# DeltaNet keys normed by the diagonal of their products, and one shared product for the last 16 tokens of eight heads

## The chip, the cores and the metric

The kernel runs on one core of a Trainium2 chip. The metric is device microseconds of one execution; lower is better. The engines are named as in the profile: PE (matrix products), PEld (its weight loads), DVE (vector), ACT (activation functions and copies), POOL, and SP, which issues most DMAs.

## The reference, cut to what matters

The block is one decoder layer on 272 tokens (16 meta tokens and 256 others), all in float32. One of its two token mixers is a chunked gated DeltaNet with 16 key and query heads and 32 value heads of 128 channels. The change touches only this part:

```python
def l2norm(x):
    return x * lax.rsqrt(jnp.sum(x * x, axis=-1, keepdims=True) + EPS)

qkv = jax.nn.silu(causal_dwconv(jnp.concatenate([q, k, v], axis=-1), conv_w)).astype(f32)
q, k, v = jnp.split(qkv, [GDN_QK_W, 2 * GDN_QK_W], axis=-1)
q = jnp.repeat(l2norm(q.reshape(B, L, GDN_QK_HEADS, Dh)), rep, axis=2) * (Dh ** -0.5)
k = jnp.repeat(l2norm(k.reshape(B, L, GDN_QK_HEADS, Dh)), rep, axis=2)
...
kk = jnp.einsum('bhid,bhjd->bhij', kc, kc)
lower = jnp.where(strict, bc[..., :, None] * kk * decay, 0.0)
...
attn = jnp.where(incl, jnp.einsum('bhid,bhjd->bhij', qc, kc) * decay, 0.0)
```

## The kernel before, in words

**The stream of weights.** Nearly all time goes to products of the activations with 376 weight tiles of 128 x 2048 (1 MB each). `Stream.load` fetches a tile on SP's queue into `wraw` (3 buffers). For each half of a tile ACT rounds it to `whi` (L149, 5 buffers) and DVE takes the rest to `wlo` (L157, 4 buffers). PE then runs 24 products of 256 to 272 columns for that half, into a PSUM tile `acc`. All matrix products are recorded at line 227 (helper `MM`), vector operations of two tensors at L230 (helper `TT`), activations at L243 (helper `ACT`).

**The background.** Everything else, the DeltaNet too, is written as generators that a list `bg` holds. `gemm` calls `bg.tick(EV)` ahead of the 24 products of a half and `bg.tick(PE)` behind them. At each tick up to five of the generators go one step. So what a generator does between two `yield`s lands either ahead of a half's products (on ACT, DVE, POOL and SP) or behind them (on PE). Each engine then runs its own instructions in the order in which they were written, and may run ahead of the others as far as data and buffers allow.

**PSUM.** The background has five PSUM tiles, `BP()` (named `bp`). Where a sixth is asked for, its first writer waits until the reader of an older one is done.

**The part that changes.** `gen_kq(h)` runs once for each of the 16 key heads, two at a time: heads 0 to 7 while the attention heads finish, at 362 to 446 us; heads 8 to 15 at 700 to 850 us. For keys (272 tokens) and queries (258) alike it squares (ACT), splits the squares into a rounded part `sqh` (ACT) and a rest `sql` (DVE), adds them up over the channels with two products by ones (PE, 272 or 258 columns), takes Ln and Exp (ACT), and multiplies (DVE). Then come the products: keys by keys (`a`, 272, 144 and 16 columns) and queries by keys (`b`, 258, 144 and 16). The products of 16 columns are for the last 16 tokens, from the third chunk. ACT copies all to `kq[h]` and `kq3`, POOL copies the diagonal 32 x 32 blocks to `ckk`.

`gen_inv(b)` runs once for eight heads. It writes `ckk` and `kq3` to memory and reads them back in another layout, inverts the triangular blocks on DVE, and writes the results for `gen_pair`, which computes the value heads in pairs.

Of the kernel before, what the change touches and what calls it, by code (L numbers as in the profile page):

```python
# [14 lines left out]
P = 128  # L15
# [192 lines left out]
def build(tc, x, w, cst, prm, out):  # L208
    nc = tc.nc
    with ExitStack() as ctx:  # L210
# [507 lines left out]
        kq3 = inv.tile([P, 8, 2, 16], F, name="kq3")  # L718
        ktl = inv.tile([P, 2, 8, 16], F, name="ktl")
        kk_dram = dram.tile([8, 2, 4, 32, 32], F, name="kk_dram")  # L720
        k3_dram = dram.tile([8, 16, 16], F, name="k3_dram")
        t_dram = [dram.tile([16, 2, 4, 32, 32], F, name=f"t_dram{b}") for b in range(2)]
        u_dram = [dram.tile([16, 2, 4, 32, 32], F, name=f"u_dram{b}") for b in range(2)]
        q3_dram = dram.tile([8, 16, 16], F, name="q3_dram")
# [41 lines left out]
        def gen_kq(h):  # L766
            k, q = raw.pop(("k", h)), raw.pop(("q", h))
            both = ((k, L, None, R("kqs")), (q, NQ, K("lnd"), R("kqs")))
            for t, n, _, s in both:
                ACT(s[:, :n], t[:, :n], AF.Square)  # L770
            yield EV
            parts = [split(s, n) for t, n, _, s in both]
            for t, n, b, s in both:
                yield PE
                p = BP()
                sums(p[:, :n], parts.pop(0))
                yield EV
                ACT(s[:, :n], p[:, :n], AF.Ln, bias=eps)
                ACT(s[:, :n], s[:, :n], AF.Exp, scale=-0.5, bias=0.0 if b is None else b)
            yield EV  # L780
            for t, n, _, s in both:
                TT(t[:, :n], t[:, :n], s[:, :n], OP.mult)
            del both, s, t
            yield EV
            while sum(("head", 2 * j + 1) not in done for j in kq) == 8:
                yield EV
            yield PE
            kq[h] = kqp.tile([P, 2, 416], F, name="kq", tag="kq")
            c = kq[h]
            a = BP()  # L790
            MM(a[:, 0:272], k[:, 0:128], k)
            MM(a[:, 272:416], k[:, 128:256], k[:, 128:272])
            MM(a[:, 416:432], k[:, 144:272], k[:, 256:272])
            yield EV
            yield from until(*[("inv", h // 8 - 1)] if h > 7 else [])
            ACT(c[:, 0, :], a[:, :416])
            ACT(kq3[96:128, h % 8, 0, :], a[96:128, 416:432])
            yield PE
            b = BP()
            MM(b[:, 14:272], k[:, 0:128], q[:, :NQ])  # L800
            MM(b[:, 272:416], k[:, 128:256], q[:, 114:258])
# [12 lines left out]
        def gen_inv(b):  # L814
# [4 lines left out]
            gb = inv.tile([P, 32], F, name="gb", tag="gb")  # L819
            nb = inv.tile([P, 32], F, name="nb", tag="nb")  # L820
# [12 lines left out]
            nc.sync.dma_start(out=k3_dram.rearrange("h j i -> j h i"), in_=kq3[112:128, :, 0, :])  # L833
            nc.sync.dma_start(out=q3_dram.rearrange("h j i -> j h i"), in_=kq3[112:128, :, 1, :])
# [6 lines left out]
            kkt = R("kkt")  # L841
            ACT(kkt[:, :256], p[:, :256])
            yield EV
            for d in range(2):
# [3 lines left out]
                nc.sync.dma_start(out=p3[h8].rearrange("p a b -> p (a b)"),  # L848
                                  in_=k3_dram.rearrange("h j i -> h (j i)"))
                nc.sync.dma_start(out=q3[h8].rearrange("p a b -> p (a b)"),  # L850
                                  in_=q3_dram.rearrange("h j i -> h (j i)"))
# [14 lines left out]
            for n, l, kk, g, be in both:  # L866
                ACT(l, l, AF.Exp)
# [7 lines left out]
            for n, l, kk, g, be in both:  # L875
# [4 lines left out]
            for n, l, kk, g, be in both:  # L880
# [574 lines left out]
```

## Time and profile before

| | |
|---|---|
| median of 3 runs | 2428.78 us (2428.12 to 2429.44) |
| the profiled execution's own time | 2428.07 us |
| its span, first to last instruction | 2426.4 us |
| PE busy | 2388.0 us (98%) |
| DVE, ACT, POOL busy | 1665.0, 1280.3, 455.0 us |
| mean granted clock of PE | 0.994 |

Busy time is the union of an engine's instructions. Products overlap on PE: a record lasts longer than the distance to the next one's start, so what a product costs is read from starts, not from durations. The span is 1.7 us shorter than the execution's own time.

### The profile page before, as it was taken

What the parts mean: (1) busy time and instruction counts of PE and PEld (TensorE: products, weight loads), DVE (VectorE), ACT (ScalarE), POOL (GpSimd) and SP (SyncE); (2) the same over time, 40 slices, a digit from 0 to 9 for tenths busy, and PEclk for the clock granted to TensorE, in tenths of its full rate; (3) what the DMA queues carried; (4) which work ended last, traced back from release to release, by engine and by line L of the source; (5) the groups of instructions that cost most, each with busy time, mean ns of one, the idle gap of its engine ahead of it and who ended that gap; (6) DMA issues with size and microseconds to landing.
All of it is one profiled execution on the core that took longest, in us unless ns stands there. A gap on an engine that the chain in (4) does not pass through costs nothing.

```text
span 2426.4 us, 48160 instructions
## 1 busy us (share of the span) xinstructions
PE 2388.0 (98%) x19870; PEld 2366.3 (98%) x19870; DVE 1665.0 (69%) x2653; ACT 1280.3 (53%) x2010; POOL 455.0 (19%) x620
## 2 busy tenths in 40 slices
PE   9999999999999999999999999999999999999997
PEld 8999999999999999999999999899999999999997
DVE  7777775796787597776665554597764777557755
ACT  6333568556767746666574544454444444334453
POOL 1767001424431134333000001210000000000012
PEclk9999999999999999999999999999999999999998
DMA  6445444564443466445676556435555455545552
GB/s 261 169 163 191 147 141 138 176 212 146 162 165 128 158 201 207 154 151 168 215 264 222 186 193 217 173 139 184 181 191 189 176 179 187 191 175 191 175 190 105
DMA packets 113836, 434.38 MB, mean 179 GB/s; under 512 B 34256, under 2 KB 63440, under 8 KB 66128
## 3 DMA queue, kind: packets, MB, share of 16 engines
q1 hardware_dynamic: 112320, 430.25, 50.9%
q8 instruction: 156, 2.56, 0.4%
q10 hardware_dynamic: 1296, 1.06, 0.1%
q14 instruction: 64, 0.52, 0.1%
HBM read 415.74 MB, written 15.52 MB: 178 GB/s over the span
## 4 chain that ended last, share of the span: by engine, by line
PE 92%; DVE 4%; ACT 3%; issue 1%; POOL 0%; DMA 0%; SPq 0%; DVEq 0%; ACTq 0%; POOLq 0%
PE acc L227 83%; PE bp L227 8%; DVE wlo L157 1%; DVE acc L230 1%; ACT whi L149 0%; ACT L243 0%; ACT sq_h L243 0%; DVE pr L230 0%; DVE tm L230 0%; ACT kqs L243 0%; PE bp L994 0%; POOL ro L230 0%; DMA wraw<-in_w_dram 0%; DVE xr L230 0%; ACT L954 0%
## 5 line engine op out<-in xcount | busy, mean ns | idle before, releaser
L157 DVE TENSOR_TENSOR wlo<-wraw,whi 128x1024 fp32r<-128x1024 f32 x747 | 932.8, 1251 | 296.7 <-PE acc L227 142.5
L149 ACT ACTIVATE whi<-wraw 128x1024 fp32r<-128x1024 f32 x747 | 786.9, 1058 | 639.6 <-PE acc L227 527.5
L227 PE MATMUL acc<-xh,whi 128*128 128x258 f32 (+3 forms) x2592 | 753.7, 291 | 5.4 <-ACT whi L138 5.4
L227 PE MATMUL acc<-xh,wlo 128*128 128x258 f32 (+3 forms) x2592 | 736.0, 284 | 0.4
L227 PE MATMUL acc<-xl,whi 128*128 128x258 f32 (+3 forms) x2592 | 733.1, 285 | 0.0
L227 PEld LDWEIGHTS acc<-xh,whi 128*128 128x128 f32 x2592 | 488.8, 189 | 7.8 <-ACT whi L138 5.4
L227 PEld LDWEIGHTS acc<-xh,wlo 128*128 128x128 f32 x2592 | 488.1, 188 | 1.3 <-DVE wlo L157 0.7
L227 PEld LDWEIGHTS acc<-xl,whi 128*128 128x128 f32 x2592 | 486.1, 188 | 1.0
L227 PE MATMUL acc<-uh,whi 128*128 128x258 f32 x1520 | 430.8, 284 | 4.4 <-ACT uh L243 2.9
L227 PE MATMUL acc<-uh,wlo 128*128 128x258 f32 x1520 | 432.5, 285 | 0.0
L227 PE MATMUL acc<-ul,whi 128*128 128x258 f32 x1520 | 429.4, 284 | 2.1 <-DVE ul L233 1.8
L227 PEld LDWEIGHTS acc<-uh,whi 128*128 128x128 f32 x1520 | 291.1, 192 | 5.2 <-ACT uh L243 3.3
L227 PEld LDWEIGHTS acc<-ul,whi 128*128 128x128 f32 x1520 | 288.1, 190 | 3.6 <-DVE ul L233 3.6
L227 PEld LDWEIGHTS acc<-uh,wlo 128*128 128x128 f32 x1520 | 289.4, 190 | 0.0
L227 PE MATMUL acc<-acth,wlo 128*128 128x256 f32 x768 | 215.9, 281 | 0.0
L227 PE MATMUL acc<-actl,whi 128*128 128x256 f32 x768 | 215.7, 281 | 0.0
L227 PE MATMUL acc<-acth,whi 128*128 128x256 f32 x768 | 215.3, 280 | 0.0
L227 PEld LDWEIGHTS acc<-acth,wlo 128*128 128x128 f32 x768 | 145.0, 189 | 0.0
L227 PEld LDWEIGHTS acc<-acth,whi 128*128 128x128 f32 x768 | 144.8, 189 | 0.0
L227 PE MATMUL acc<-oh,whi 128*128 128x258 f32 x512 | 144.8, 283 | 0.0
L227 PEld LDWEIGHTS acc<-actl,whi 128*128 128x128 f32 x768 | 144.8, 188 | 0.0
L227 PE MATMUL acc<-oh,wlo 128*128 128x258 f32 x512 | 144.6, 282 | 0.0
(325 smaller groups left out, 3610.4 us busy)
## 6 DMA issues: line engine op xcount, KB each, us to landing
wraw<-in_w_dram SPq DMA_DIRECT2D x371, 1024.0 KB
grow_h<-g_dram SPq DMA_DIRECT2D x32, 136.0 KB
s_o<-o_h SPq DMA_DIRECT2D x32, 129.0 KB
back<-s_o SPq DMA_DIRECT2D x32, 129.0 KB
wraw<-in_w_dram SPq DMA_DIRECT2D x5, 512.0 KB
s_ao<-ao SPq DMA_DIRECT2D x16, 129.0 KB
s_ga<-gate SPq DMA_DIRECT2D x16, 129.0 KB
s_gg<-gate SPq DMA_DIRECT2D x16, 129.0 KB
```

The source lines that it names most:

```text
L149: self.nc.scalar.activation(self.h[s], self.part(s), AF.Copy)
L157: self.nc.vector.tensor_tensor(out=lo, in0=self.part(s), in1=hi.bitcast(F), op=OP.subtract)
L227: nc.tensor.matmul(o, lhsT=l, rhs=r, start=start, stop=stop)
L230: (eng or nc.vector).tensor_tensor(out=o, in0=a, in1=b, op=op)
```

## The change

The keys are no longer multiplied by their norm ahead of the products. Square, split, sums, Ln, Exp and multiplication are done for the queries alone. The products of the raw keys are taken, and the sum of squares of each key is read off the diagonal of keys by keys: DVE multiplies the two diagonal blocks by the identity and reduces them. ACT makes `rk` of it, one factor for each token, and puts it in as the scale of the copies from PSUM, one copy for each of the two chunks of rows (four copies of a head instead of two). That scales rows only; the factor of the columns goes into `ntok` (POOL) and, for the inversion, into one more multiplication.

The products of 16 columns go. POOL copies the last 16 tokens of keys and queries of eight heads side by side into `last`, and `gen_inv` takes one product of 128 x 256 of it; the 16 x 16 blocks on its diagonal are what is wanted, and are picked out by the DMA's access pattern (`same`). `rk` travels to the inversion's layout through memory (`rk_dram`, `r3_dram`).

```diff
         def gen_kq(h):
             k, q = raw.pop(("k", h)), raw.pop(("q", h))
-            both = ((k, L, None, R("kqs")), (q, NQ, K("lnd"), R("kqs")))
-            for t, n, _, s in both:
-                ACT(s[:, :n], t[:, :n], AF.Square)
-            yield EV
-            parts = [split(s, n) for t, n, _, s in both]
-            for t, n, b, s in both:
-                yield PE
-                p = BP()
-                sums(p[:, :n], parts.pop(0))
-                yield EV
-                ACT(s[:, :n], p[:, :n], AF.Ln, bias=eps)
-                ACT(s[:, :n], s[:, :n], AF.Exp, scale=-0.5, bias=0.0 if b is None else b)
-            yield EV
-            for t, n, _, s in both:
-                TT(t[:, :n], t[:, :n], s[:, :n], OP.mult)
-            del both, s, t
-            yield EV
+
+            s = R("kqs")
+            ACT(s[:, :NQ], q[:, :NQ], AF.Square)
+            yield EV
+            parts = split(s, NQ)
+            yield PE
+            p = BP()
+            sums(p[:, :NQ], parts)
+            del parts
+            yield EV
+            ACT(s[:, :NQ], p[:, :NQ], AF.Ln, bias=eps)
+            ACT(s[:, :NQ], s[:, :NQ], AF.Exp, scale=-0.5, bias=K("lnd"))
+            del p
+            yield EV
+            TT(q[:, :NQ], q[:, :NQ], s[:, :NQ], OP.mult)
+            del s
             while sum(("head", 2 * j + 1) not in done for j in kq) == 8:
                 yield EV
+            yield from until(*[("inv", h // 8 - 1)] if h > 7 else [])
+            nc.gpsimd.tensor_copy(out=last[:, 0, h % 8, :], in_=k[:, 256:272])
+            nc.gpsimd.tensor_copy(out=last[:, 1, h % 8, :], in_=q[:, 242:258])
             yield PE
             kq[h] = kqp.tile([P, 2, 416], F, name="kq", tag="kq")
             c = kq[h]
-            a = BP()
+            a, b = BP(), BP()
             MM(a[:, 0:272], k[:, 0:128], k)
             MM(a[:, 272:416], k[:, 128:256], k[:, 128:272])
-            MM(a[:, 416:432], k[:, 144:272], k[:, 256:272])
-            yield EV
-            yield from until(*[("inv", h // 8 - 1)] if h > 7 else [])
-            ACT(c[:, 0, :], a[:, :416])
-            ACT(kq3[96:128, h % 8, 0, :], a[96:128, 416:432])
-            yield PE
-            b = BP()
             MM(b[:, 14:272], k[:, 0:128], q[:, :NQ])
             MM(b[:, 272:416], k[:, 128:256], q[:, 114:258])
-            MM(b[:, 416:432], k[:, 144:272], q[:, 242:258])
-            yield EV
-            ACT(c[:, 1, 14:416], b[:, 14:416])
-            ACT(kq3[96:128, h % 8, 1, :], b[96:128, 416:432])
+            del k, q
+            yield EV
+            t = R("diag")
+            for i in range(2):
+                TT(t[:, 128 * i:128 * i + 128], a[:, 272 * i:272 * i + 128], ident, OP.mult)
+            nc.vector.tensor_reduce(out=rk[:, h, :], in_=t[:, :256].rearrange("p (t c) -> p t c", t=2), axis=AX.X, op=OP.add)
+            del t
+            yield EV
+            ACT(rk[:, h, :], rk[:, h, :], AF.Ln, bias=eps)
+            ACT(rk[:, h, :], rk[:, h, :], AF.Exp, scale=-0.5)
+            for i, sl in enumerate((slice(0, 272), slice(272, 416))):
+                ACT(c[:, 0, sl], a[:, sl], scale=rk[:, h, i:i + 1])
+            for i, sl in enumerate((slice(14, 272), slice(272, 416))):
+                ACT(c[:, 1, sl], b[:, sl], scale=rk[:, h, i:i + 1])
+            del a, b
+            n = ntok[:, :, 2 * h:2 * h + 2]
+            TT(n, n, rk[:, h, :, None].to_broadcast([P, 2, 2]), OP.mult, nc.gpsimd)
...
             nc.sync.dma_start(out=kk_dram.rearrange("h t b j i -> (b j) h t i"), in_=ckk)
-            nc.sync.dma_start(out=k3_dram.rearrange("h j i -> j h i"), in_=kq3[112:128, :, 0, :])
-            nc.sync.dma_start(out=q3_dram.rearrange("h j i -> j h i"), in_=kq3[112:128, :, 1, :])
+            nc.sync.dma_start(out=rk_dram.rearrange("h t p -> p h t"), in_=rk[:, 8 * b:8 * b + 8, :])
             yield PE
...
+            MM(p[:, 256:512], last[:, 0].rearrange("p h c -> p (h c)"), last.rearrange("p t h c -> p (t h c)"))
+            yield EV
+            kkt, kqt = R("kkt"), R("kqt")
             ACT(kkt[:, :256], p[:, :256])
+            TT(kqt[:, :128], p[:, 256:384], ident, OP.mult)
+            nc.vector.tensor_reduce(out=r3, in_=kqt[:, :128], axis=AX.X, op=OP.add)
+            yield EV
+            ACT(r3, r3, AF.Ln, bias=eps)
+            ACT(r3, r3, AF.Exp, scale=-0.5)
+            ACT(kqt[:, :256], p[:, 256:512], scale=r3)
+            del p
+            nc.sync.dma_start(out=kt_dram, in_=kqt[:, :256])
+            nc.sync.dma_start(out=r3_dram, in_=r3)
...
                 TT(l, l, be[:, :, None].to_broadcast(sh), OP.mult)
+                TT(l, l, r[:, None, :].to_broadcast(sh), OP.mult)
```

The first place is PE, heads 8 and 9, the step of the products. Before, one step held keys by keys of both heads, and queries by keys came a half later (`bp_9557` and `bp_9562` are the two `a`):

```order
L227 MATMUL bp_9553<-vb_9232,nn_9344 128x128
L227 MATMUL bp_9557<-kraw_8721 128x272 [waits PE_49]
L227 MATMUL bp_9557<-kraw_8721 128x144
L227 MATMUL bp_9557<-kraw_8721 128x16
L227 MATMUL bp_9562<-kraw_8939 128x272
L227 MATMUL bp_9562<-kraw_8939 128x144
L227 MATMUL bp_9562<-kraw_8939 128x16
L227 MATMUL acc_9508<-xh_297,whi_9355 128x272
```

Now (`bp_9446` and `bp_9453` are the two `a`, `bp_9447` and `bp_9454` the two `b`):

```order
L227 MATMUL bp_9442<-vb_9136,nn_9223 128x128
L227 MATMUL bp_9446<-kraw_8750 128x272 [waits PE_49]
L227 MATMUL bp_9446<-kraw_8750 128x144
L227 MATMUL bp_9447<-qraw_8848,kraw_8750 128x258 [waits DVE_49,PE_49]
L227 MATMUL bp_9447<-qraw_8848,kraw_8750 128x144
L227 MATMUL bp_9453<-kraw_8951 128x272 [waits PE_49,Activation_49]
L227 MATMUL bp_9453<-kraw_8951 128x144
L227 MATMUL bp_9454<-qraw_9080,kraw_8951 128x258 [waits DVE_49,PE_49,Activation_49]
L227 MATMUL bp_9454<-qraw_9080,kraw_8951 128x144
```

The products of 16 columns are gone, and the two heads now fill four PSUM tiles in one step.

The second place is the half behind it, where a pair of value heads of `gen_pair` needs three PSUM tiles (two for its sums by ones, one for its next product). On PE now:

```order
L227 MATMUL bp_9517<-sqh_9467,oner_87 128x258 [waits Activation_49]
L227 MATMUL bp_9517<-sql_9468,oner_87 128x258 [waits DVE_49]
L227 MATMUL bp_9518<-sqh_9471,oner_87 128x258 [waits Activation_49]
L227 MATMUL bp_9518<-sql_9472,oner_87 128x258 [waits DVE_49]
L227 MATMUL bp_9523<-d2_9475,u_9078 128x128 [waits Activation_49]
```

and on ACT, in the turn that follows, the readers of these tiles and of the four of the heads:

```order
L243 ACTIVATE sq_h_9460<-bp_9517,eps_85 128x258 [waits PE_49]
L243 ACTIVATE sq_h_9460<-sq_h_9460 128x258 [waits Activation_49]
L243 ACTIVATE sq_h_9464<-bp_9518,eps_85 128x258 [waits PE_49]
L243 ACTIVATE sq_h_9464<-sq_h_9464 128x258 [waits Activation_49]
L243 ACTIVATE rk_632<-rk_632,eps_85 128x2 [waits DVE_49]
L243 ACTIVATE rk_632<-rk_632 128x2 [waits Activation_49]
L243 ACTIVATE kq_9445<-bp_9446,rk_632 128x272 [waits Activation_49]
```

The four tiles of the heads are read only behind the two Ln of the pair. Before, ACT read the two `a` ahead of the pair's Ln (this is ACT before, at the same step):

```order
L243 ACTIVATE kq_9556<-bp_9557 128x416 [waits PE_49]
L243 ACTIVATE kq3_631<-bp_9557 32x16
L243 ACTIVATE kq_9561<-bp_9562 128x416 [waits PE_49]
L243 ACTIVATE kq3_631<-bp_9562 32x16
L149 ACTIVATE whi_9592<-wraw_9307 128x1024
L243 ACTIVATE sq_h_9567<-bp_9620,eps_85 128x258 [waits PE_49]
```

So in that half the pair's three tiles now share the one PSUM tile that the two heads leave free. Before, the two `a` had been read by then, and the pair's three tiles and the two `b` filled the five.

The third place is SP's queue behind the eighth head, from the write of `ckk` to the next load of weights. Before, and then now:

```order
L832 DMA kk_dram_633<-ckk_630 128x16x32 [waits DMAHW6_49,Pool_49]
L833 DMA k3_dram_634<-kq3_631 16x8x16 [waits DMAHW7_49,Activation_49]
L834 DMA q3_dram_639<-kq3_631 16x8x16 [waits DMAHW0_49,Activation_49]
L1114 DMA s_ga_596<-gate_5569 128x258 [waits DMAHW1_49,DVE_49]
L120 DMA wraw_5576<-in_w_dram 128x2048 [waits DMAHW2_49,DVE_49]
```

```order
L843 DMA kk_dram_634<-ckk_630 128x16x32 [waits DMAHW2_49,Pool_49]
L844 DMA rk_dram_635<-rk_632 128x16x1 [waits DMAHW3_49,Activation_49]
L1139 DMA s_ga_596<-gate_5405 128x258 [waits DMAHW4_49,DVE_49]
L120 DMA wraw_5412<-in_w_dram 128x2048 [waits DMAHW5_49,DVE_49]
L862 DMA kt_dram_636<-kqt_5443 128x256 [waits DMAHW6_49,DVE_49,Activation_49]
L863 DMA r3_dram_637<-small_5209 128x1 [waits DMAHW7_49]
```

The two writes of 256 pieces in all became one of 2048 pieces of 4 bytes ahead of the load, and two more writes behind it.

## Rows read from the trace of the kernel before

**Rows 1.** The page: busy time by engine, and the chain that ended last.

```profile
PE 2388.0 (98%) x19870; PEld 2366.3 (98%) x19870; DVE 1665.0 (69%) x2653; ACT 1280.3 (53%) x2010; POOL 455.0 (19%) x620
...
PE 92%; DVE 4%; ACT 3%; issue 1%; POOL 0%; DMA 0%; SPq 0%; DVEq 0%; ACTq 0%; POOLq 0%
```

**Rows 2.** Busy time in stretches: PE, PEld, DVE, ACT, POOL, clock, DMA, GB/s.

```profile
362.00:446.00 84.00, 82.03 (x636) 79.73 (x636) 45.96 (x83) 64.34 (x140) 16.64 (x76) 1.00 0.44 139
...
788.00:852.00 64.00, 63.62 (x503) 62.14 (x502) 35.79 (x56) 46.98 (x87) 10.51 (x49) 1.00 0.49 161
```

**Rows 3.** What PE waited for, 360 to 860 us: total, times, longest.

```profile
PE bp L227 <- ACT pt L243: 1.1, 1, 1.1
PE bp L227 <- ACT d L243: 1.0, 1, 1.0
```

**Rows 4.** Timeline of PE, keys by keys of two heads: start, duration, instruction.

```profile
434.98 0.28 PE L227 MATMUL acc<-xh,wlo 128*128 128x258 f32 x1
435.10 1.92 PE L227 MATMUL bp<-kraw 128*128 128x272 f32 x12
...
437.07 0.29 PE L227 MATMUL acc<-xl,whi 128*128 128x258 f32 x1
```

**Rows 5.** Timeline of PE, an indexer head's products of 144 and 272 columns.

```profile
80.09 0.28 PE L227 MATMUL acc<-xh,wlo 128*128 128x256 f32 x1
80.21 0.86 PE L227 MATMUL bp<-krik,iqr 128*128 128x144 f32 x4
...
81.03 0.28 PE L227 MATMUL acc<-xl,whi 128*128 128x256 f32 x1
```

**Rows 6.** Timeline of PE: the sums of two heads' keys, on time.

```profile
418.80 0.28 PE L227 MATMUL acc<-xh,wlo 128*128 128x258 f32 x1
...
419.42 0.28 PE L227 MATMUL acc<-xh,whi 128*128 128x258 f32 x1
```

**Rows 7.** Timeline of PE: two products of 256 columns in the inversion.

```profile
512.77 0.29 PE L227 MATMUL acc<-xh,wlo 128*128 128x272 f32 x1
512.89 1.02 PE L227 MATMUL bp<-wbd,kkt 128*128 128x256 f32 x4
...
513.87 0.28 PE L227 MATMUL acc<-xl,whi 128*128 128x258 f32 x1
```

**Rows 8.** Timeline of PE: the sums of two heads' keys, late, twice.

```profile
798.28 0.29 PE L227 MATMUL acc<-xh,wlo 128*128 128x272 f32 x1
...
799.77 0.28 PE L227 MATMUL acc<-xh,whi 128*128 128x272 f32 x1
...
827.04 0.28 PE L227 MATMUL acc<-xh,wlo 128*128 128x258 f32 x1
...
828.37 0.28 PE L227 MATMUL acc<-xh,whi 128*128 128x258 f32 x1
```

**Rows 9.** ACT, groups by shape, 360 to 860 us: busy, mean ns, idle before.

```profile
L243 ACT ACTIVATE kqs<-bp,eps 128x272 f32<-128x272 f32 x16 | 7.7, 479 | 0.7 <-PE bp L227 0.5
L243 ACT ACTIVATE sq_h<-bp,eps 128x258 f32<-128x258 f32 x16 | 7.5, 469 | 9.8 <-PE bp L227 9.8
...
L243 ACT ACTIVATE sqh<-kqs 128x272 fp32r<-128x272 f32 x16 | 6.8, 425 | 1.8 <-DMA s_ao<-ao 1.7
...
L243 ACT ACTIVATE kq<-bp 32x16 f32<-32x16 f32 x32 | 5.7, 177 | 0.6
```

**Rows 10.** DVE, groups by shape, 230 to 860 us.

```profile
L230 DVE TENSOR_TENSOR sql<-kqs,sqh 128x272 fp32r<-128x272 f32 x16 | 7.1, 442 | 18.4 <-ACT sqh L243 16.5 <-PE bp L227 1.9
...
L230 DVE TENSOR_TENSOR z<-bp,nbtok 32x128 f32<-32x128 f32 x16 | 4.7, 291 | 2.1 <-PE bp L227 1.7
```

**Rows 11.** Timelines of SP and ACT: writes, a load of weights, its first reader.

```profile
440.73 0.89 SPq L833 DMA_DIRECT2D k_dram<-kq  x1
...
443.39 0.37 SPq L120 DMA_DIRECT2D wraw<-in_w_dram  x1
...
453.50 1.06 ACT L149 ACTIVATE whi<-wraw 128x1024 fp32r<-128x1024 f32 x1 [0.50 <-ACT l L243]
```

More of the change, by code (lines that the diff above doesn't have):

```diff
@@ L717, in build @@
         ckk = inv.tile([P, 8, 2, 32], F, name="ckk")
-        kq3 = inv.tile([P, 8, 2, 16], F, name="kq3")
+        last = inv.tile([P, 2, 8, 16], F, name="last")
+        rk = inv.tile([P, 16, 2], F, name="rk")
         ktl = inv.tile([P, 2, 8, 16], F, name="ktl")
         kk_dram = dram.tile([8, 2, 4, 32, 32], F, name="kk_dram")
-        k3_dram = dram.tile([8, 16, 16], F, name="k3_dram")
+        rk_dram = dram.tile([8, 2, P], F, name="rk_dram")
+        kt_dram = dram.tile([P, 256], F, name="kt_dram")
+        r3_dram = dram.tile([P, 1], F, name="r3_dram")
         t_dram = [dram.tile([16, 2, 4, 32, 32], F, name=f"t_dram{b}") for b in range(2)]
         u_dram = [dram.tile([16, 2, 4, 32, 32], F, name=f"u_dram{b}") for b in range(2)]
-        q3_dram = dram.tile([8, 16, 16], F, name="q3_dram")
         w3_dram = [dram.tile([16, 16, 16], F, name=f"w3_dram{b}") for b in range(2)]
@@ L818, in gen_inv @@
             tm = inv.tile([P, 32, 32], F, name="tm", tag="tm")
-            gb = inv.tile([P, 32], F, name="gb", tag="gb")
-            nb = inv.tile([P, 32], F, name="nb", tag="nb")
+            small = R("small")
+            gb, nb, rb = (small[:, a:a + 32] for a in (0, 32, 64))
+            r16, ei, r3 = small[:16, 96:112], small[:16, 112:128], small[:, 128:129]
             l3, p3, x3, q3 = (R(n)[:16, :256].rearrange("p (a b) -> p a b", a=16) for n in ("l3", "p3", "x3", "q3"))
@@ L839, in gen_inv @@
                 nc.tensor.transpose(p[:, 128 * i:128 * i + 128], ktl[:, i].rearrange("p h c -> p (h c)"), ident)
+            MM(p[:, 256:512], last[:, 0].rearrange("p h c -> p (h c)"), last.rearrange("p t h c -> p (t h c)"))
             yield EV
-            kkt = R("kkt")
+            kkt, kqt = R("kkt"), R("kqt")
             ACT(kkt[:, :256], p[:, :256])
+            TT(kqt[:, :128], p[:, 256:384], ident, OP.mult)
+            nc.vector.tensor_reduce(out=r3, in_=kqt[:, :128], axis=AX.X, op=OP.add)
             yield EV
+            ACT(r3, r3, AF.Ln, bias=eps)
[6 more added lines that the diff above has]
+            yield EV
+            same = lambda x: bass.AP(tensor=kt_dram[:].tensor, offset=kt_dram[:].offset + x,
+                                     ap=[[16 * 256 + 16, 8], [256, 16], [1, 16]])
             for d in range(2):
@@ L847, in gen_inv @@
                                   in_=kk_dram.rearrange("h t b j i -> (h t b) (j i)"))
[L848 to L851, printed above, removed]
+                nc.sync.dma_start(out=rb[half], in_=rk_dram.rearrange("h t (x i) -> (h t x) i", i=32))
+                nc.sync.dma_start(out=p3[h8], in_=same(0))
+                nc.sync.dma_start(out=q3[h8], in_=same(128))
+                nc.sync.dma_start(out=r16[h8], in_=r3_dram.rearrange("(h c) o -> h (c o)", h=8))
             yield EV
-            ei = inv.tile([16, 16], F, name="ei", tag="ei")
             TS(ei, g3[:, 0, 1:], g3[:, 0, 0:1], 0.0, OP.subtract, OP.min)
-            both = ((32, lm, pr, gb, nb), (16, l3, p3, g3[:, 0, 1:], g3[:, 1, 1:]))
-            for n, l, kk, g, be in both:
+            both = ((32, lm, pr, gb, nb, rb), (16, l3, p3, g3[:, 0, 1:], g3[:, 1, 1:], r16))
+            for n, l, kk, g, be, r in both:
                 sh = [P if n == 32 else 16, n, n]
@@ L865, in gen_inv @@
             ACT(ei, ei, AF.Exp)
-            for n, l, kk, g, be in both:
+            TT(ei, ei, r16, OP.mult, nc.gpsimd)
+            for n, l, kk, g, be, r in both:
                 ACT(l, l, AF.Exp)
@@ L873, in gen_inv @@
                                     base=0, channel_multiplier=0)
-            for n, l, kk, g, be in both:
+            for n, l, kk, g, be, r in both:
                 sh = [P if n == 32 else 16, n, n]
@@ L878, in gen_inv @@
                 TT(l, l, be[:, :, None].to_broadcast(sh), OP.mult)
+                TT(l, l, r[:, None, :].to_broadcast(sh), OP.mult)
             yield EV
-            for n, l, kk, g, be in both:
+            for n, l, kk, g, be, r in both:
                 nc.gpsimd.affine_select(out=l, in_=l, pattern=[[1, n], [-1, n]], compare_op=OP.is_gt, fill=0.0,
```

## The prediction, made before the changed kernel ran

> **What bounds the kernel now.** I read the page first: PE is busy 98% of the span and makes up 92% of the chain that ended last [rows 1]. So work taken off PE shortens the kernel one for one, and work moved to or from another engine counts only where PE stands and waits for it. Next I read the stretches in which the changed code runs: the granted clock is 1.00 in both, the upper of its two levels, 2.4 GHz, so one price holds for all products, and of the other engines ACT is the busiest (64.3 of 84 us, 77%, then 73%), DVE 55% [rows 2]. Last the list of what PE waits for: between 360 and 860 us its largest entries are 1.1 and 1.0 us, both on ACT [rows 3]. That column misses part of what is lost (below), so I price waits from starts, too: on time, a product of the stream starts 0.12 us after the one before.
>
> **What leaves PE.** (1) The products of 16 columns. A float32 product is two records. From the last stream product ahead of the block to the second one behind it keys by keys of two heads take 437.07 − 434.98 = 2.09 us [rows 4]; less two stream products of 0.12 that is 1.85. An indexer head has the same products of 144 and 272 columns and none of 16: 81.03 − 80.09 = 0.94, less two of 0.118, 0.70 [rows 5]. So 1.85 − 2 x 0.70 = 0.45 us is the price of two products of 16 columns, 0.22 each, or 0.11 a pass. There are 32 (16 heads, keys and queries): 32 x 0.22 = 7.0 us. (2) The keys' sums, two products of 272 columns for each head: four of them take 419.42 − 418.80 − 0.12 = 0.50 us where nothing is late, 0.125 each [rows 6]; 32 x 0.125 = 4.0 us. (3) What is added: in each of the two inversions one product of 256 columns. Two such take 513.87 − 512.77 − 0.245 = 0.855 us [rows 7], so 0.43 each, 0.9 us in all. Net 7.0 + 4.0 − 0.9 = 10.1 us less on PE.
>
> The price of (1) is where a formula would mislead. The rows give 0.11 us for a pass of 16 columns [rows 4, 5]. The Trainium skill (TensorE: Matmul & The Clock Gate, Back-to-back issue gap) gives for a single matmul at 2.4 GHz N/2.4 + 2.5 ns, 9 ns for 16 columns, by which the 64 passes would be worth 0.6 us and the change 3.7 us on PE. The same page says of the formula that it leaves out the weight load at small N, and puts a load of 128 columns at 128/1.2 = 107 ns (section LDWEIGHTS): 6.8 us for 64. The rows agree with the load, not with the gap.
>
> **Waits that become shorter.** Squares and split of both heads of a step stand ahead of the keys' sums, on ACT and DVE, in one turn. Two blocks that hold just the sums show PE late: 799.77 − 798.28 = 1.49 us where 0.125 + 0.50 is due, 0.87 lost, and 828.37 − 827.04 = 1.33 where 0.62 is due, 0.71 lost [rows 8]. Two earlier blocks, at 381 and 730 us, have the same order ahead of them, and I count them alike. Afterwards the queries' sums stand in this place, and half of the squares and splits ahead are gone. For two heads that frees at least two splits of 0.425 on ACT [rows 9], and the last rest that PE needs is the second on DVE, no longer the third, 0.44 earlier [rows 10]. So at least 0.44 of each loss goes and at most all: I take 0.6 for each of four, 2.4 us (bounds 0 and 3.2). For the two ACT waits of 1.1 and 1.0 [rows 3] I take nothing: the work that they wait behind changes places, but ACT has less of it, so up to 2.1 more could go.
>
> **ACT, DVE, POOL.** Per head ACT loses four operations on 272 columns (0.43 to 0.48 each, the split and Ln in rows 9) and two small copies of 0.177, and gains two small operations and two more copies' fixed parts, each near the 0.177 of the smallest copy: about 1.4 us less, 23 us in all. It hides behind PE and counts only in the waits above. DVE loses 0.44 for the rest and about as much for the multiplication, and gains two multiplications of 128 columns from PSUM (0.29 is the nearest, `z`) and a reduction of 256, bounded by 0.29 and 0.44: 0.9 against 0.9 to 1.0 [rows 10], nothing. If DVE were behind, the multiplication of the queries would be what PE waits for: it now stands in the same half as the product that reads it, before one half ahead. It has the stream's 24 products (2.9 us) and keys by keys (0.7) to be done; I take 0, with 0.5 for each of eight steps as bound were DVE a whole rest of weights late. POOL's copies into `last` are read by PE only in the inversion. That gains one turn, a multiplication of its large tile and a round trip of `rk`; DVE does it between rests of weights while PE runs the stream, and if it ended late the value heads would start a half later, with the same work for PE.
>
> **A wait that is added: PSUM tiles.** Two heads now hold four of the five tiles for two halves, until ACT has copied all with their scales. Where a pair of value heads runs beside them, at heads 8 and 9, the pair's two sums and its next product share the fifth tile: the second sum can't start until ACT has taken the first through Ln, and the product not until Ln of the second. Behind PE stand the stream's next products, so this is lost outright. Priced from rows: first sum 0.24 plus 0.16 until it is out (a record of 0.28 [rows 6] less the 0.12 to the next start); Ln 0.47 [rows 9]; second sum 0.40; Ln 0.47. The product starts 1.75 us after the first sum instead of 0.48, some 1.3 us late, with the hand-overs 1.4. Four more instructions wait for such a reader (the sums beside three older tiles at 390 us, a `b` at 420 us, and `a` and `b` of head 9), but they have 2 to 3 us of PE's other work ahead of them and ACT's reader needs 0.4 to 0.8: I take 0 for these, up to 1.0 each if ACT is behind.
>
> **Sum.** 10.1 off PE, 2.4 of waits gone, 1.4 of waits new: 11.1 us less. The profiled execution took 2428.07 us, the span and 1.7 around it, so 2417.0; the median of the three runs lies 0.7 above it, so 2417.7. What 0.2% is, 4.9 us, is about what a measurement of this kernel can tell from no change.
>
> **Rivals.** (A) New waits eat the old ones' gain and more: the five PSUM waits cost 1.4 + 4 x 1.0, and the sums stay as late as they are. Then 10.1 − 5.4 = 4.7 us less, 2424.1. For it: ACT is the busiest of the others there (77%) [rows 2], and waits on ACT are the longest [rows 3]. Against it: ACT loses some 1.4 us a head. What lies between this and the forecast counts as A. (B) The waits around the heads go altogether, 3.2 + 2.1 us, and the pair's products are late by no more than their own 1.4: 14 us less, 2414.8; without that wait 2413.4. (C) A 16-column product costs PE next to nothing, since its load hides behind others: then PE sheds 4.0 − 0.9 = 3.1, with the waits 4.1 us, 2424.7, no change that could be told. The two readings against each other, 1.85 and 2 x 0.70, speak against it [rows 4, 5]. The formula cited above is this case. (D) Slower: the weights come late. `rk` goes to memory in 2048 pieces of 4 bytes on SP's queue, right ahead of a load of weights. The longest issue of the small writes takes 0.89 us for 128 pieces [rows 11]; were it to grow with the pieces, 16 times, SP would be held for 14 us in each inversion. A load there is read 453.50 − 443.39 = 10.1 us after its issue, and ACT's rounding is four halves, some 12 us, ahead of PE. So it decides from about 22 us: beyond that PE stops one for one, and each inversion would need 22 + 8 = 30 us to make the kernel slower by over 4.9 us (11.1 + 4.9 in two parts). At 14 us it costs nothing. The Trainium skill (DMA: Bandwidth & Descriptors, Specifications) names 512 bytes as the least for full rate, which speaks for slow pieces, not for how slow; no row shows 4-byte pieces alone.
>
> **Chances.** Forecast, 2414.5 to 2421: 0.76. A, 2421 to 2424: 0.09. B, below 2414.5: 0.08. C: 0.03. D: 0.02. That the trade of work leaves the time within 0.2% in some other way, 0.02. So faster by over 0.2% (below 2423.9) 0.92, within it 0.06, slower 0.02. The range for 8 in 10 is 2413.5 to 2422.
>
> **What would show it.** In the trace after: 64 records of 16 columns for `kraw` gone, 32 sums of 272 columns gone, four records of 128 x 256 for `last` added; the block of products of two heads takes near 2.75 us (2 x 0.70 and 2 x 0.67). The queries' sums late by less than 0.4 us per block. The pair beside heads 8 and 9 with gaps of 0.5 to 0.8 us ahead of its second sum and of the product behind it. From the second inversion's end on, PE as before. I am wrong if the blocks without 16 columns aren't shorter by 0.45 per two, if PE shows waits on `kq`'s copies or on `diag` in more than the places named, or if PE waits for a DMA.

## The result, and the profile after

The changed kernel takes 2441.85 us (median of 4 runs, 2441.18 to 2443.07) against 2428.88 (4 runs, 2428.12 to 2429.44) before: ratio 1.0055, interval 1.004 to 1.007. It is 13.0 us slower where 11.1 less was forecast.

The page of the changed kernel, beside [rows 1]: busy time by engine, the chain that ended last, and its largest links.

```profile
PE 2388.1 (98%) x19778; PEld 2366.6 (97%) x19778; DVE 1668.4 (68%) x2677; ACT 1263.7 (52%) x1984; POOL 486.1 (20%) x670
...
PE 88%; DVE 5%; DMA 2%; ACT 2%; POOL 1%; issue 1%; SPq 0%; DVEq 0%; ACTq 0%; POOLq 0%
PE acc L227 80%; PE bp L227 8%; DVE wlo L157 2%; DMA pr<-kk_dram 1%; DMA grow_h<-g_dram 1%; DVE acc L230 1%; POOL dc L240 1%; DVE pr L230 0%; DVE tm L230 0%; ACT whi L149 0%; ACT sq_h L243 0%; ACT L243 0%; ACT L979 0%; POOL ro L230 0%; PE b
```

PE has 92 records less and is as busy as before, so those that are left took longer. The chain lost 4 points of PE, and DMA, which had none, has 2: `pr<-kk_dram` is a read-back of the inversion. Now the stretches where heads run, as in [rows 2], and the two inversions (columns as there).

```profile
362.00:446.00 84.00, 84.00 (x658) 82.38 (x658) 51.31 (x101) 57.88 (x130) 25.36 (x99) 1.00 0.57 130
788.00:852.00 64.00, 64.00 (x515) 63.41 (x515) 40.39 (x66) 43.91 (x79) 19.21 (x61) 1.00 0.57 148
425.00:513.00 88.00, 80.29 (x611) 78.86 (x610) 68.83 (x124) 35.84 (x47) 24.64 (x40) 0.94 0.67 163
842.00:928.00 86.00, 79.19 (x610) 78.41 (x609) 66.60 (x121) 32.02 (x39) 27.42 (x41) 0.94 0.70 173
```

Where the heads run PE is full now (84.00 of 84 us, 82.03 before). In each inversion it stands for 7 to 8 us, and the granted clock is 0.94. What PE waits for, over the whole span (total, times, longest), two entries; before, the first stood at 0.9 us (the third line) and the second was not there:

```profile
PE acc L227 <- DVE wlo L157: 10.2, 7, 3.6
...
PE acc L227 <- ACT whi L149: 5.1, 2, 2.6
```

```profile
PE acc L227 <- DVE wlo L157: 0.9, 1, 0.9
```

PE waits for weights, and the weights for SP and the DMA. SP's timeline from the end of the eighth head (start, us, instruction), and the two readers of these weights on ACT:

```profile
424.90 0.85 SPq L844 DMA_DIRECT2D rk_dram<-rk  x1
...
427.13 0.39 SPq L120 DMA_DIRECT2D wraw<-in_w_dram  x1
427.62 0.37 SPq L862 DMA_DIRECT2D kt_dram<-kqt  x1
428.04 0.42 SPq L863 DMA_DIRECT2D r_dram<-small  x1
...
432.81 1.86 SPq L120 DMA_DIRECT2D wraw<-in_w_dram  x1
...
438.21 0.45 SPq L872 DMA_DIRECT2D small<-rk_dram  x1
448.64 0.30 SPq L873 DMA_DIRECT2D p<-kt_dram  x1
...
454.45 0.38 SPq L120 DMA_DIRECT2D wraw<-in_w_dram  x1
```

```profile
442.10 2.01 ACT L149 ACTIVATE whi<-wraw 128x1024 fp32r<-128x1024 f32 x2 [10.43 <-PE acc L227]
...
452.58 2.00 ACT L149 ACTIVATE whi<-wraw 128x1024 fp32r<-128x1024 f32 x2 [7.12 <-DMA wraw<-in_w_dram]
```

The issue of `rk`'s 2048 pieces took 0.85 us, no more than one of 128 before (0.89) [rows 11]. But the load behind it was read 15.0 us after its issue (10.1 before) and the next one 19.8 us after. (The profile names PE for the first of ACT's two waits. But PE ran on at its usual pace until 450.8 and frees a buffer of ACT's every 2.9 us, 24 products of 0.12, so I take it that the load came last there too.) Meanwhile SP stood at the read-back of `rk` until 438.21, 13.3 us after the write was issued, and at that of `kt` until 448.64, 21.0 after; and the following weights were issued only at 454.45. What PE lost is more than its standing, as windows of 4 us show (columns as in [rows 2]):

```profile
448.00:452.00 4.00, 3.05 (x25) 2.83 (x23) 0.00 (x0) 0.00 (x0) 0.00 (x0) 1.00 0.65 183
452.00:456.00 4.00, 1.87 (x6) 1.55 (x7) 2.33 (x3) 2.00 (x2) 0.70 (x1) 0.63 0.57 102
456.00:460.00 4.00, 4.00 (x19) 4.00 (x19) 3.90 (x5) 0.00 (x0) 2.89 (x3) 0.52 0.80 302
460.00:464.00 4.00, 1.46 (x9) 1.24 (x8) 3.97 (x6) 2.00 (x2) 3.22 (x2) 0.91 0.76 279
464.00:468.00 4.00, 4.00 (x24) 4.00 (x24) 3.79 (x12) 2.31 (x3) 3.37 (x9) 0.66 0.85 281
```

After PE had stood, its granted clock fell to 0.52, near the lower level, 1.2 GHz: 19 products in 4.00 busy us, against 25 in 3.05 at a clock of 1.00.

### The profile page after: what moved, and what is told of

It is laid out like the page before. It is cut to its first block, busy times and chain, and to the rows that moved or that the text cites. A ratio compares the mean times of both kernels' runs of the same rounds, so it can differ in the third digit from the quotient of the medians.

```text
span 2440.4 us, 48019 instructions
## 1 busy us (share of the span) xinstructions
PE 2388.1 (98%) x19778; PEld 2366.6 (97%) x19778; DVE 1668.4 (68%) x2677; ACT 1263.7 (52%) x1984; POOL 486.1 (20%) x670
## 4 chain that ended last, share of the span: by engine, by line
PE 88%; DVE 5%; DMA 2%; ACT 2%; POOL 1%; issue 1%; SPq 0%; DVEq 0%; ACTq 0%; POOLq 0%
PE acc L227 80%; PE bp L227 8%; DVE wlo L157 2%; DMA pr<-kk_dram 1%; DMA grow_h<-g_dram 1%; DVE acc L230 1%; POOL dc L240 1%; DVE pr L230 0%; DVE tm L230 0%; ACT whi L149 0%; ACT sq_h L243 0%; ACT L243 0%; ACT L979 0%; POOL ro L230 0%; PE bp L1019 0%
## 5 line engine op out<-in xcount | busy, mean ns | idle before, releaser
L227 PE MATMUL acc<-xh,whi 128*128 128x258 f32 (+3 forms) x2592 | 758.9, 293 | 10.8 <-ACT whi L138 5.7
L227 PEld LDWEIGHTS acc<-xh,wlo 128*128 128x128 f32 x2592 | 492.7, 190 | 11.4 <-DVE wlo L157 10.8
```

The source lines that it names most:

```text
L227: nc.tensor.matmul(o, lhsT=l, rhs=r, start=start, stop=stop)
```

## The experiments

Theories, before them: **pieces**, the many small writes hold up the transfers behind them; **read-backs**, SP stands at the read-backs and so issues weights late; **rest**, the heads' new waits. What a run lost in an inversion is given, for its profiled execution, as the time from start to start of PE's products less what these products take when nothing is late (by the distances of [rows 4 to 7]): 13.3 and 11.8 us in the changed kernel, 0.5 and 0 before. All ratios are to the kernel before on the same chip (2428.4 to 2429.0 us).

**1. `rk` in 16 pieces of 512 bytes**, turned by a transpose on PE first:

```diff
-nc.sync.dma_start(out=rk_dram.rearrange("h t p -> p h t"), in_=rk[:, 8 * b:8 * b + 8, :])
+nc.tensor.transpose(pk[:16, :128], rk[:, 8 * b:8 * b + 8, :].rearrange("p h t -> p (h t)"), ident)
+ACT(rkt[:16, :128], pk[:16, :128])
+nc.sync.dma_start(out=rk_dram.rearrange("h t p -> (h t) p"), in_=rkt[:16, :128])
```

> The changed kernel, but rk is turned by one product of PE (128 x 16 to 16 x 128) and copied by ACT, so that its write to memory has 16 pieces of 512 bytes in place of 2048 of 4 bytes. All waits of SP's queue and the order of its read-backs stay. If the small pieces are what makes the weights late (theory 'pieces'), the 25 us that PE loses in the two inversions go, and the time is 2415 to 2419 us. If SP is held because it stands at the read-backs while loads of weights queue behind (theory 'read-backs'), most stays: 2430 to 2442 us.

2422.94 us, ratio 0.9979 (0.9969 to 0.9988): between the two ranges. 19 us of 24 come back. But 4.3 us are still lost in the first inversion, and SP still stands, at `kt`'s read-back until 440.51.

**2. The read-backs six turns later**, pieces of 4 bytes kept:

```diff
+for _ in range(6):
+    yield EV
 same = lambda x: bass.AP(tensor=kt_dram[:].tensor, offset=kt_dram[:].offset + x,
```

> The changed kernel with the read-backs of the inversion six turns (some 18 us) later, and rk still in pieces of 4 bytes. By 'pieces' the loads of weights issued behind rk's write still land 15 to 20 us after their issue, so PE still loses at least 5 us in each inversion: 2427 to 2438 us. By 'read-backs' SP no longer stands, the weights come in time: 2415 to 2420 us.

2424.63, ratio 0.9985 (0.9975 to 0.9994): between the two. 6.8 and 6.1 us are lost in the inversions, about half of what the changed kernel loses.

**3. `rk`'s write on ACT's queue:**

```diff
-nc.sync.dma_start(out=rk_dram.rearrange("h t p -> p h t"), in_=rk[:, 8 * b:8 * b + 8, :])
+nc.scalar.dma_start(out=rk_dram.rearrange("h t p -> p h t"), in_=rk[:, 8 * b:8 * b + 8, :])
```

> The changed kernel with rk's write, still 2048 pieces of 4 bytes, issued on ACT's DMA queue in place of SP's. If the pieces hold up only what stands behind them in the same queue, the weights pass them and the time is 2415 to 2422 us. If they hold up the DMA engines whatever the queue, it stays at 2430 to 2442 us. By 'read-backs' it also stays there, since SP must still wait for the write.

2431.41, ratio 1.0014 (1.0004 to 1.0024), 6.9 and 6.2 us lost: another queue gives back 10 of 24 us, but the pieces slow transfers that don't share theirs: run 1, which differs only in how `rk` is written (16 pieces, on SP's queue), is 8.5 us faster. The Trainium skill (DMA: Bandwidth & Descriptors, Issuing engines are not separate DMA queues) says that all queues end on the same 16 engines; this run agrees.

**4. The kernel before with a write that nobody reads**, 2048 pieces of 4 bytes, side by side in memory, behind `ckk`'s:

```diff
+dm_dram = dram.tile([16, P], F, name="dm_dram")
 nc.sync.dma_start(out=kk_dram.rearrange("h t b j i -> (b j) h t i"), in_=ckk)
+nc.sync.dma_start(out=dm_dram.rearrange("x p -> p x"), in_=kc[:, 0:16])
```

> The kernel before with one more write on SP's queue in each of the two inversions, behind that of ckk: 2048 pieces of 4 bytes of a constant to a place that nothing reads; the results stay the same. By 'pieces' it alone delays the weights, by 5 to 12 us for PE in each inversion: 2438 to 2453 us. By 'read-backs' it costs nothing beyond its issue: 2428 to 2431 us.

2435.21, ratio 1.0027 (1.0016 to 1.0038). The write costs 6.8 us in a kernel where nothing else changed: too much for *read-backs* (up to 2431), less than *pieces* wanted (2438 and more).

**5 and 6. The same, each piece 64 bytes from the next, and pieces of 128 bytes**, a copy of `ckk`'s write:

```diff
+dm_dram = dram.tile([16, P, 16], F, name="dm_dram")
+nc.sync.dma_start(out=dm_dram[:, :, 0:1].rearrange("x p o -> p x o"), in_=kc[:, 0:16][:, :, None])
```

```diff
+dm_dram = dram.tile([8, 2, 4, 32, 32], F, name="dm_dram")
+nc.sync.dma_start(out=dm_dram.rearrange("h t b j i -> (b j) h t i"), in_=ckk)
```

> The kernel before with a write of 2048 pieces of 4 bytes in each inversion that nothing reads, as in the run with the dummy write, but each piece 64 bytes from the next. If the price is that of small pieces as such: the same loss as there, 2432 to 2438 us. If the price comes from neighbouring pieces that fall into the same 64 bytes of memory: it is gone, 2428 to 2430 us.

> The kernel before with the keys' blocks written a second time in each inversion to memory that nothing reads: 2048 pieces of 128 bytes, as many pieces as the 4-byte write had. If the price goes by the number of pieces: as there, 2432 to 2438 us. If it is the 4 bytes: 2427 to 2430 us.

2428.66, ratio 1.0000 (0.9991 to 1.0009), and 2428.98, 1.0002 (0.9992 to 1.0011). So neither the number of pieces nor their 4 bytes is enough to cost time here; what differs in run 4 is how they lie, side by side. Run 5 also spreads them over 128 KB in place of 8, and no run separates the one from the other. The Trainium skill (DMA: Bandwidth & Descriptors, Specifications) names one bound, 512 bytes, as the least for full rate, with a read-modify-write below it. The pieces of runs 4, 5 and 6 all lie below it, and only run 4 loses time, so that bound does not tell them apart.

**7. Repairs of 1 and 2 together:** to the edit of run 1 this is added.

```diff
+for _ in range(3):
+    yield EV
```

> Two repairs at once: rk is turned on TensorE and written in 16 pieces of 512 bytes, and the read-backs are issued 3 turns later. If the loss of the changed kernel is the 4-byte pieces and SyncE's stand at the read-backs together, both are gone, and what is left is the change of TensorE's work: 2415 to 2420 us, PE without waits of over 0.5 us on the split weights in both inversions. If something else of the change keeps the weights late (the 64-byte read-backs of kt themselves, say), it stays near the first repair alone, 2421 to 2425 us.

2433.80, ratio 1.0022 (1.0012 to 1.0031): a miss on both sides. The inversions lose just 2.6 and under 0.3 us, but PE then waits for the pair of value heads behind them (here behind the first; 3.7 and 2.0 us behind the second):

```profile
PE bp L227 <- ACT d L243: 4.4, 1, 4.4
...
PE bp L227 <- DVE nn L230: 1.1, 1, 1.1
```

**8. The shared product alone**: keys normed as before, `k3_dram` and `q3_dram` replaced by `kt_dram`, the read-backs one turn later than before.

```diff
-MM(a[:, 416:432], k[:, 144:272], k[:, 256:272])
-MM(b[:, 416:432], k[:, 144:272], q[:, 242:258])
+MM(p[:, 256:512], last[:, 0].rearrange("p h c -> p (h c)"), last.rearrange("p t h c -> p (t h c)"))
```

> The kernel before with the shared product alone: keys normalised as before, the 32 products of 16 columns replaced by one of 256 columns for each inversion (kt written and read back, 1 turn later than before, no rk). If a product of 16 columns costs its 0.22 us on TensorE as the forecast took it: 32 x 0.22 less 0.9, so 2421.5 to 2424 us. If those products were nearly free (the rival that they hide): 2427 to 2430 us. If SyncE's stand at kt's read-back costs here too: 2424 to 2427 us, with waits on the split weights in the inversions.

2435.16, ratio 1.0026 (1.0016 to 1.0036): a miss, with waits of 2.9 (`d`) and 1.8 us behind the first inversion, 0.9 and 1.8 behind the second. SP's timeline shows the same thing as in run 7: the write of the inverse comes behind three loads, which SP can only issue as buffers come free. First this run, then run 9, which has it one turn earlier:

```profile
508.17 13.05 SPq L120 DMA_DIRECT2D wraw<-in_w_dram  x3
521.27 0.42 SPq L921 DMA_DIRECT2D t_dram<-tm  x1
```

```profile
506.64 5.47 SPq L120 DMA_DIRECT2D wraw<-in_w_dram  x2
512.16 0.42 SPq L920 DMA_DIRECT2D t_dram<-tm  x1
```

**9. As 8, with no turn added**, `kt`'s write and read-backs issued by GpSimd (edit against run 8):

```diff
-nc.sync.dma_start(out=kt_dram, in_=kqt[:, :256])
-for _ in range(2):
-    yield EV
+nc.gpsimd.dma_start(out=kt_dram, in_=kqt[:, :256])
+yield EV
```

> The kernel before with the shared product alone and not one turn more than before has, kt written and read back by GpSimd. If the run of this part with a later read-back was slow because the inversion ended later and its pairs of value heads came closer together: those waits are gone, and the price of the 32 products of 16 columns shows, 2421 to 2424 us. If the shared product or kt's way through memory costs it: 2430 to 2437 us, as there. If products of 16 columns are nearly free and nothing else happens: 2427 to 2429 us.

2421.73, ratio 0.9970 (0.9958 to 0.9982). The product alone is worth 6.9 us (6.1 forecast: 7.0 less 0.9), and run 8 is 13 us slower by one turn and by the queue. That the queue isn't it is argued from run 13, where it makes no difference in another kernel. So run 2's late read-backs were no clean test either.

**10. As 1, `kt` and `r3` written and read back by GpSimd**, in the turns of the changed kernel:

```diff
-nc.sync.dma_start(out=p3[h8], in_=same(0))
+nc.gpsimd.dma_start(out=p3[h8], in_=same(0))
```

> The run with rk written in 512-byte pieces, with the write of kt and r3 and their read-backs issued by GpSimd in the same turns as before, so that SyncE no longer stands at them. If SyncE's stand at kt's read-back (433.6 to 440.5 us there) is what still delayed weights: the 4.3 us of waits on the split weights in the first inversion go, 2416 to 2421 us. If it is the pieces of the read-backs, or the turns of the pairs behind the inversion: 2421 to 2426 us, with the wait of the first pair of value heads still there.

2428.66, ratio 1.0001 (0.9991 to 1.0010): above both ranges and worse than run 1, though SP no longer stood at `kt`'s read-back. 6.6 and 5.5 us are lost in the inversions. So SP's standing is not what was left in run 1, and *read-backs* alone is no account of the loss; why this run is worse stays open. While the slow writes are there, SP's late issues may still have a share: run 2, where the loads go ahead of the read-backs, loses half.

**11. The changed kernel with `rk`'s pieces 64 bytes apart:**

```diff
-rk_dram = dram.tile([8, 2, P], F, name="rk_dram")
+rk_dram = dram.tile([8, 2, P, 16], F, name="rk_dram")
+nc.sync.dma_start(out=rk_dram[:, t, :, 0:1].rearrange("h p o -> p h o"), in_=rk[:, 8 * b:8 * b + 8, t, None])
```

> The changed kernel with nothing but rk's place in memory changed: its 2048 pieces of 4 bytes are still written one by one, each 64 bytes from the next (two transfers of 1024 pieces), and read back from there. If the loss comes from neighbouring pieces in the same 64 bytes: about as the run with 512-byte pieces, 2420 to 2427 us. If it comes from 4-byte pieces as such, or from SyncE waiting for the read-backs whatever they are: 2435 to 2444 us.

2436.10, ratio 1.0032 (1.0021 to 1.0043): 6 us less than the changed kernel. That is in the range of small pieces as such or of SP's waiting; if only neighbours cost, 15 to 22 us less were expected. But the run changes more than `rk`'s neighbours, and leaves others: `r3`, too, is written in pieces of 4 bytes side by side, 128 of them, and `rk` is now read by single 4 bytes. The next runs take these up.

**12. As 1, with `r3` as a 257th column of `kt`**, in `kt`'s own pieces:

```diff
-nc.sync.dma_start(out=kt_dram, in_=kqt[:, :256])
-nc.sync.dma_start(out=r3_dram, in_=r3)
+nc.sync.dma_start(out=kt_dram[:, :257], in_=kqt[:, :257])
```

> The run with rk in 512-byte pieces, and the last tokens' scales r3 no longer written as 128 neighbouring pieces of 4 bytes: they go out as a 257th column of kt, in the same pieces. No neighbouring 4-byte writes are left. If these hold the transfers up (few of them too): the low stretch of 40 to 76 GB/s around 433 to 440 us goes, and with it waits on the split weights, 2414 to 2420 us. If SyncE's stand at kt's read-back is the rest of the loss: about 2421 to 2425 us, as without this step.

2418.15 (4 runs, 2418.04 to 2418.83), ratio 0.9957 (0.9942 to 0.9972). No write of neighbouring 4 bytes is left, and the forecast's time is there within 0.5 us; on this chip it is 10.4 us less than before (2428.51), 11.1 forecast. SP reads `kt` back 5.8 us after its write was issued, 21.0 in the changed kernel (SP's timeline, run 12):

```profile
427.96 0.32 SPq L867 DMA_DIRECT2D kt_dram<-kqt  x1
...
433.71 0.30 SPq L877 DMA_DIRECT2D p<-kt_dram  x1
434.12 0.29 SPq L878 DMA_DIRECT2D q<-kt_dram  x1
```

From the product of `last` to that of `wbd` PE runs the same products in both, run 12 one transpose more. The changed kernel, then run 12:

```profile
424.32 0.60 PE L227 MATMUL bp<-last 128*128 128x256 f32 x2
...
511.30 1.03 PE L227 MATMUL bp<-wbd,kkt 128*128 128x256 f32 x4
```

```profile
424.72 0.60 PE L227 MATMUL bp<-last 128*128 128x256 f32 x2
...
500.21 1.03 PE L227 MATMUL bp<-wbd,kkt 128*128 128x256 f32 x4
```

86.98 us against 75.49: 11.5 of the 23.7 us between the two kernels, and the second inversion gives 84.95 against 73.2, 11.7.

**13. As 12, `kt` written and read back by GpSimd** (the read-backs as in run 10):

```diff
-nc.sync.dma_start(out=kt_dram[:, :257], in_=kqt[:, :257])
+nc.gpsimd.dma_start(out=kt_dram[:, :257], in_=kqt[:, :257])
```

> As the run with r3 in kt's pieces, with kt's write and the three read-backs of it issued by GpSimd, so that SyncE doesn't stand at them. If SyncE's stand costs by itself: 1 to 4 us less than that run, 2413 to 2418 us. If it costs nothing once no neighbouring 4-byte pieces are left: the same as that run within 1 us.

2417.53 (2414.58 to 2420.99), ratio 0.9954 (0.9939 to 0.9969). Run 12's times lie within this spread: without the slow writes, SP's standing (5.8 us in run 12) costs nothing that can be told. This is the fastest version here, with run 12.

**14. The changed kernel with the edit of run 12 alone**, `rk` in its 2048 pieces.

> The changed kernel with r3 in kt's pieces alone, rk still written in 2048 neighbouring pieces of 4 bytes. If rk's write is the larger part and r3's the smaller: 2433 to 2439 us, the loss in both inversions smaller than the 13.3 and 11.8 us of the changed kernel. If r3's write behind rk's is what keeps SyncE standing: 2424 to 2430 us. If it is nothing: 2440 to 2443 us.

2434.63, ratio 1.0024 (1.0015 to 1.0033): 7.2 us come back; 7.7 and 6.0 us are still lost in the inversions of the profiled execution, at 2430.55 the fastest of ten.

**15. The kernel before with `r3`'s write**, 128 neighbouring pieces that nobody reads:

```diff
+dm_dram = dram.tile([P, 1], F, name="dm_dram")
+nc.sync.dma_start(out=dm_dram, in_=kc[:, 0:1])
```

> The kernel before with a write of 128 neighbouring pieces of 4 bytes in each inversion that nothing reads, as r3's. If neighbouring pieces cost by their number: a sixteenth of what 2048 cost, nothing to be seen, 2428 to 2429 us. If a few already hold the engines up: 2430 to 2434 us.

2429.30, ratio 1.0001 (0.9992 to 1.0011): nothing in the time. But the DMA's own view shows it. Busy share of the 16 engines in tenths and GB/s, 40 slices of 1 us from 424 us on. First GB/s of the kernel before, without such a write:

```profile
GB/s 426 100 1 198 188 344 418 33 0 99 66 147 401 426 57 0 0 157 114 74 197 131 369 414 227 180 215 121 147 451 434 132 131 254 401 262 0 0 0 0
```

Run 15, written at 440.59:

```profile
DMA  9409599303748920097390595728699995989980
GB/s 393 117 1 222 106 254 459 139 0 122 92 66 336 475 107 0 0 177 94 105 166 0 49 49 25 49 33 213 254 379 217 240 230 139 377 352 394 467 369 33
```

Run 4, 2048 of them at 440.66, and run 5, 64 bytes apart at 440.48:

```profile
DMA  9408589203569920099692879935587899936898
GB/s 418 125 1 198 123 319 442 98 0 105 84 82 401 410 115 0 0 163 103 19 84 2 12 25 58 40 33 42 58 147 213 340 287 203 217 98 135 328 401 323
```

```profile
DMA  9219788003549910099589799989858899940000
GB/s 391 29 56 175 188 369 369 25 0 132 74 106 401 401 66 16 0 196 71 20 163 158 123 319 365 254 188 213 165 119 262 369 385 460 393 188 8 0 0 0
```

The changed kernel, written at 424.90 and 428.04:

```profile
DMA  0798979899946496999948365659412929999955
GB/s 0 122 143 56 54 7 27 37 54 67 57 25 57 82 156 254 373 415 120 51 49 53 94 131 146 234 128 225 126 27 54 201 33 385 385 404 425 410 199 81
```

With 128 neighbours the transfers are at 0 to 49 GB/s for six slices (445 to 451 us; 131 to 414 before), with 2048 at 2 to 84 for ten (443 to 453 us), while the engines are shown as busy for half to two thirds of the time; 64 bytes apart there is no such stretch. In the changed kernel it is eleven slices at 7 to 82, with both writes in it. In the kernel before, six slices are covered by the weights ahead; in the changed one eleven, with SP's late issues behind them, are not.

**16. Run 12 with `r3`'s old write put back**, which nobody reads:

```diff
 nc.sync.dma_start(out=kt_dram[:, :257], in_=kqt[:, :257])
+nc.sync.dma_start(out=dm_dram, in_=kqt[:, 256:257])
```

> The run with r3 in kt's pieces and no loss, plus r3's old write of 128 neighbouring pieces of 4 bytes, which nothing reads any more. If the write itself is what the step before gained by removing: back to 2421 to 2425 us, with a stretch of low GB/s of some 6 us. If it was the read-back of r3 that cost: 2417.5 to 2419.5 us.

2424.88, ratio 0.9981 (0.9972 to 0.9990): 6.7 us worse than run 12. It is the write, not its read-back. The same 128 pieces cost nothing in run 15: what a slow stretch costs depends on what waits behind it. Here SP stands at `kt`'s read-back until 440.64 (433.71 in run 12).

**17. Run 11 with the edit of run 12.**

> The run with rk's 4-byte pieces 64 bytes apart, and r3 in kt's pieces: no neighbouring 4-byte writes are left, but 2048 single ones and their read-backs by 4 bytes are. If only neighbours cost: 2417 to 2423 us. If r3's write was no part of that run's loss and small pieces cost wherever they lie: 2430 to 2440 us.

2425.26, ratio 0.9983 (0.9973 to 0.9992): 10.8 us less than run 11 and 9.4 less than run 14, whose pieces are neighbours, but 7.1 more than run 12, and between the two ranges. What is left is single pieces, written and read back by 4 bytes. Written alone they cost nothing in the kernel before (run 5), so I put it on the read-backs. No run separates the two, but SP's timeline speaks for it: it issues `rk`'s read-back as early as run 12 does (432.83 there), and only what stands behind it is late (`q`'s read-back at 434.12 there):

```profile
432.51 0.55 SPq L872 DMA_DIRECT2D small<-rk_dram  x1
...
441.54 0.31 SPq L874 DMA_DIRECT2D q<-kt_dram  x1
```

## Why the prediction was wrong

The step that failed is the price of rival D. It took the first cost of 2048 small pieces to be SP's time to issue them, scaled it by their number from the longest issue [rows 11], and found 14 us hidden behind 22. The issue took 0.85 us, no more than the 0.89 of 128 pieces; what grew is how long the transfers behind it take. Two things in it were missed. The time from the issue of a load of weights to its reading was taken to be as before, and it went from 10.1 to 15.0 and 19.8 us. And SP, which waits at the read-backs of these very writes, then issued the next weights late: the slack of 22 us was used from both ends. Together that cost PE 13.3 and 11.8 us, where D, at its own 14 us of issue, had nothing. Slowness of the write itself is shown (runs 4, 15, 16), and that it goes with pieces side by side (4 against 5). SP's standing cost nothing once the slow writes were gone (13 against 12); what share its late issues have beside them is not separated (runs 2 and 10). D's chance of 0.02 rested on that one price; no row of before had neighbouring 4-byte writes, so its upper bound should have been open and the range with it. `r3`'s 128 pieces were not priced at all, and they cost 6.7 us (16 against 12).

The rest of the sum held, as run 12 shows, where the two writes are replaced: 2418.15 against 2417.7. That it comes so near is in part luck. Two waits that the sum took to stay went, and two came that it did not have; run 12's list of what PE waits for, whole span, has the latter and the new PSUM wait:

```profile
PE acc L227 <- DVE wlo L157: 1.8, 2, 0.9
PE bp L227 <- DVE nn L230: 1.5, 1, 1.5
...
PE bp L227 <- ACT sq_h L243: 1.1, 2, 0.6
```

- **Products of 16 columns**: 7.0 less 0.9 forecast; 6.9 measured for that part alone (run 9; any wait that came or went with it is in the 6.9). The block of two heads takes 418.24 − 415.45 − 0.12 = 2.67 us (2.75 forecast) in the changed kernel's timeline of PE, so rival C falls:

```profile
415.45 0.28 PE L227 MATMUL acc<-xh,wlo 128*128 128x258 f32 x1
415.57 0.87 PE L227 MATMUL bp<-kraw 128*128 128x272 f32 x4
...
418.24 0.38 PE L227 MATMUL acc<-xh,whi 128*128 128x258 f32 x1
```

- **Late sums**: 0.6 of each loss was to go; nearly all goes. From 800.31 to 800.91 four sums are on time, 5 x 0.12, where [rows 8] had lost 0.87.

```profile
800.31 0.29 PE L227 MATMUL acc<-xh,wlo 128*128 128x272 f32 x1
...
800.91 0.29 PE L227 MATMUL acc<-xh,whi 128*128 128x272 f32 x1
```

- **The two waits on ACT** (`pt` and `d`, 1.1 and 1.0 us [rows 3]): nothing was taken for them, and both are gone, in the changed kernel and in run 12. So around the heads rival B was right, with some 2.1 us more than the forecast.

- **The new PSUM wait**: gaps of 0.5 to 0.8 us forecast, 0.57 twice measured. The pair's product starts 753.79 − 751.74 = 2.05 us after the first sum, not 0.48: 1.57 late, 1.3 to 1.4 forecast. The four other waits don't show, as taken.

```profile
751.74 0.28 PE L227 MATMUL bp<-sqh,oner 128*128 128x258 f32 x1
...
752.72 0.39 PE L227 MATMUL bp<-sqh,oner 128*128 128x258 f32 x1 [0.57 <-ACT sq_h L243]
...
753.79 0.71 PE L227 MATMUL bp<-d,u 128*128 128x128 f32 x4 [0.57 <-ACT sq_h L243]
```

- **Not foreseen**: a wait of 0.9 us on `wlo` in the first inversion of run 12, and one of 1.5 us on `nn` behind it (1.6 in run 13), because the inversion now ends earlier against PE's products or its data later; which, stays open.

## What to carry to other kernels

A small transfer that a change adds is priced by what it does to the transfers behind it, on every queue, and by who waits for its landing, not by its bytes or its issue. Don't write scalars to memory as 4-byte pieces side by side: turn them so that a row goes out whole, or append them to a larger row. To set them 64 bytes apart is not enough where they are read back one by one (run 17, 7.1 us). And a step put one turn later can fall behind a load that waits for a buffer: look at what it then queues behind.

## What the hardware showed that was not expected

Behind one write of 128 pieces of 4 bytes, 512 bytes in all, the 16 DMA engines moved 0 to 49 GB/s for six us, and behind 2048 pieces 2 to 84 GB/s for ten; behind 2048 of them 64 bytes apart, or 2048 of 128 bytes, there was no such stretch. Distances between 4 and 64 bytes, pieces between 4 and 128, and pieces apart within the same 8 KB were not tried, and the mechanism in memory is not shown.
